# A mixture-of-experts layer on one core: the experts' combine with an unweighted one-hot, and rows in two fp32r parts

## The chip, the cores and the metric

The kernel runs as one program on one core of one Trainium2 chip. Five engines work side by side: TensorE (PE; its weight loads are listed as PEld), VectorE (DVE), ScalarE (ACT), GpSimd (POOL) and SyncE (SP), which in this kernel issues the transfers of weights. The metric is device time of one execution in microseconds (us), the median of several runs. All times below are from runs of this kernel or from the trace of one profiled execution.

## The reference, cut to what matters

One transformer layer on 256 tokens of width 2048, in fp32: a token mixer (window attention and a gated delta rule), then a hierarchical mixture of 32 experts, of which each token uses two. The mixer is not touched by the change. Of the experts this matters:

```python
combine = jnp.sum(jax.nn.one_hot(expert_idx, N_EXPERTS) * weights[..., None], axis=1)   # 256 x 32
y = jnp.zeros((n, d), jnp.float32)
for e in range(N_EXPERTS):
    gate, up = jnp.split(t @ w_gate_up[e], 2, axis=-1)                                   # 2048 -> 2 x 512
    y = y + combine[:, e:e + 1] * ((jax.nn.silu(gate) * up) @ w_down[e])                 # 512 -> 2048
x = layer_norm(ALPHA * x + g2 * y, ln2_g, ln2_b)
```

## The kernel before, in words

The experts are worked on in 16 pairs, one after the other. Each expert has 64 slots for tokens, so a pair fills the 128 partitions. For each pair TensorE does this:

- `gather`: the normalized rows of the pair's tokens, `xh`, are fetched into slots by a product with a one-hot matrix `G` (token by slot, two tiles of 128 tokens). The results `xg` become `XT` on ACT and DVE.
- `gate_up`: 16 loads of weights of 1 MB, `w_gu`; for each the products `pg` and `pu`, at line 1161, four records each. (A plain fp32 product shows as two records in the trace.)
- `turned`: `hs` = silu(gate) x up is turned around (`ht`, then copied to `hT`).
- `down`: 8 loads of 1 MB, `w_dn`, in four chunks `c` of 512 columns, two loads each. The product `pd` (line 1197) is followed by `dn` = `pd` x `g2b` on DVE (line 1201, `g2b` is the row g2), and by the combine: for each of the two token tiles the product `cb` (line 1207) of `GT` and `dn`, which DVE adds to `x` (line 1211, for the first pair 1209).
- `back`: `GT` is the transposed one-hot, in which each one is the token's weight: `Gw` = `G` x `comb` on DVE (line 1128), turned by TensorE (`gt`, line 1129), copied to SBUF (line 1130).

A chunk's combine isn't emitted right behind its `pd`: `down` appends it to the list `pend`, and `settle()` emits it behind the next chunk's `pd`, the last chunk's in the next pair's `gate_up`. The next pair's `gather` and `back` stand between `gate_up` and `down`. A scheduler then mixes neighbouring steps a little, and fixes the order of each engine. Each engine does its instructions in that order.

The loads go through SP's one queue into 17 buffers of 1 MB: 4 of the tile `w` (line 77), 6 of `w2` (line 1224) and 7 of `w1` (line 1239), in turn. SP issues a load when the buffer's last product is done. A pair needs 24 loads. In the first two stages of the kernel, before about 860 us, weights are split in two fp32r parts and multiplied in three products (`mm3`, lines 267 to 269); `mx` is one of their outputs. `last_rows` (line 1330) sets up the final layer norm's rows `l` during the last pair. If an expert has more than 64 tokens, a loop behind the pairs works them off (`overflow`).

Of the kernel before, what the change touches and what calls it, by code (L numbers as in the profile page):

```python
# [9 lines left out]
F32 = mybir.dt.float32  # L10
F32R = mybir.dt.float32r
AF = mybir.ActivationFunctionType
ALU = mybir.AluOpType
AX = mybir.AxisListType
PSUM = bass.MemoryType.PSUM

P = 128
D = 2048
KT = D // P
S = 256  # L20
NT = S // P
# [4 lines left out]
NE = 32  # L26
# [3 lines left out]
CAP = 64  # L30
# [36 lines left out]
def tile_block(ctx: ExitStack, tc: tile.TileContext, A: dict, out: bass.AP, dbg=None, upto=99):  # L67
# [40 lines left out]
    ident, ones = C("ident"), C("ones")  # L108
# [247 lines left out]
    def hilo(h, lo, src):  # L356
        SC.copy(h, src)
        V.tensor_tensor(lo, src, h.bitcast(F32), op=SUB)
# [725 lines left out]
    def weights():  # L1084
# [10 lines left out]
        V.tensor_add(o1, o1, o2)  # L1095
        over_groups(comb, o1)

    cnt = mo.tile([P, NE], F32, name="cnt")
    cmax = mo.tile([P, 1], mybir.dt.int32, name="cmax")
    cmaxf = mo.tile([P, 1], F32, name="cmaxf")  # L1100
# [13 lines left out]
    def slots(pr, pos2):  # L1114
        Gs = []
        for t in range(NT):
            Gt = mo.tile([P, 2, CAP], F32, tag=f"G{t}", name=f"G{pr}_{t}")
            V.tensor_tensor(Gt, pos2[:, t, :].unsqueeze(2).to_broadcast([P, 2, CAP]),
                            C("iom").unsqueeze(1).to_broadcast([P, 2, CAP]), op=ALU.is_equal)
            Gs.append(Gt)  # L1120
        return Gs

    def back(pr, Gs, comb2):
        GT = mo.tile([P, NT, P], F32, tag="GT", name=f"GT{pr}", bufs=2)
        p = pm(f"gt{pr}")
        for t in range(NT):
            Gw = mo.tile([P, 2, CAP], F32, tag=f"Gw{t}", name=f"Gw{pr}_{t}")
            V.tensor_tensor(Gw, Gs[t], comb2[:, t, :].unsqueeze(2).to_broadcast([P, 2, CAP]), op=MUL)
            T.transpose(p[:, t * P:(t + 1) * P], Gw.rearrange("p e s -> p (e s)"), ident)
        V.tensor_copy(GT, p[:, :S].rearrange("p (t s) -> p t s", t=NT))  # L1130
        return GT

    def gather(pr, Gs):
        XT = mo.tile([P, KT, P], F32, tag="XT", name=f"XT{pr}")

        def step(kq):
            p = pm(f"xg{pr}_{kq}")
            for k in range(4):
                for t in range(NT):
                    T.matmul(p[:, k * P:(k + 1) * P], xh[t][:, (4 * kq + k) * P:(4 * kq + k + 1) * P],  # L1140
                             Gs[t].rearrange("p e s -> p (e s)"), start=(t == 0), stop=(t == NT - 1))
            for k in range(4):
                K = 4 * kq + k
                if kq % 2:
                    V.tensor_scalar(XT[:, K, :], p[:, k * P:(k + 1) * P], sc2c[:, K:K + 1], sh2c[:, K:K + 1],
                                    op0=MUL, op1=ADD)
                else:
                    SC.activation(XT[:, K, :], p[:, k * P:(k + 1) * P], AF.Identity, bias=sh2c[:, K:K + 1],  # L1148
                                  scale=sc2c[:, K:K + 1])
        return XT, step  # L1150
# [32 lines left out]
    def settle():  # L1183

        while pend:
            pend.pop(0)()

    def down(pr, hT, GT, load):

        for c in range(4):  # L1190
            cs = slice(c * 512, (c + 1) * 512)
            pd = ps_d.tile([P, 512], F32, tag="d", name=f"pd{pr}_{c}")
            for fh in range(2):
                we = load(c, fh)
                for f in (2 * fh, 2 * fh + 1):
                    for e in range(2):
                        T.matmul(pd[64 * e:64 * e + 64, :], hT[:, f, 64 * e:64 * e + 64],  # L1197
                                 we[:, (2 * (f % 2) + e) * 512:(2 * (f % 2) + e + 1) * 512],
                                 start=(f == 0), stop=(f == 3))
            dn = mo.tile([P, 512], F32, tag="dn", name=f"dn{pr}_{c}", bufs=2)  # L1200
            V.tensor_tensor(dn, pd, g2b[:, cs], op=MUL)  # L1201
            settle()

            def add(c=c, cs=cs, dn=dn):
                for t in range(NT):
                    p = pm(f"cb{pr}_{c}{t}")
                    T.matmul(p, GT[:, t, :], dn, start=True, stop=True)  # L1207
                    if pr == 0:
                        V.scalar_tensor_tensor(x[t][:, cs], x[t][:, cs], ALPHA, p, op0=MUL, op1=ADD)
                    else:  # L1210
                        V.tensor_tensor(x[t][:, cs], x[t][:, cs], p, op=ADD)  # L1211
                    if pr == NE // 2 - 1:
                        V.bn_stats(sd[:, t, c, :], x[t][:, cs])

            pend.append(add)
# [39 lines left out]
        return w  # L1255

    def pair(pr):
        return pos[:, :, 2 * pr:2 * pr + 2], comb[:, :, 2 * pr:2 * pr + 2]

    def overflow():  # L1260
        NU = 3 * (NE // 2)
        ov = mo
        rp = ov.tile([P, NT, 3 * NE], F32, name="ov_pos")
        rc = ov.tile([P, NT, 3 * NE], F32, name="ov_comb")
        need = ov.tile([P, NU], F32, name="ov_need")
        pc = ov.tile([P, NE // 2], F32, name="ov_pc")
        V.tensor_reduce(pc, cnt.rearrange("p (a b) -> p a b", b=2), axis=AX.X, op=ALU.max)
        for r in range(3):
            V.tensor_scalar(rp[:, :, NE * r:NE * (r + 1)], pos, float(CAP * (r + 1)), None, op0=ALU.subtract)
            V.tensor_copy(rc[:, :, NE * r:NE * (r + 1)], comb)  # L1270
            V.tensor_scalar(need[:, 16 * r:16 * r + 16], pc, float(CAP * (r + 1)), None, op0=ALU.is_gt)
        pf = [ov.tile([P, NU], F32, name=f"ov_pf{j}") for j in range(2)]
        V.tensor_copy(pf[0], need)
        for j in range(6):
            d = 1 << j
            a, b = pf[j % 2], pf[(j + 1) % 2]
            V.tensor_copy(b[:, :d], a[:, :d])
            V.tensor_tensor(b[:, d:], a[:, d:], a[:, :NU - d], op=ALU.add)
        incl, eq = pf[0], pf[1]
        nn = ov.tile([P, 1], mybir.dt.int32, name="ov_n")  # L1280
        V.tensor_copy(nn, incl[:, NU - 1:NU])
        V.tensor_tensor(incl, incl, need, op=ALU.subtract)
        pid = C("pid")
        V.tensor_scalar(eq, incl, pid, None, op0=ALU.is_equal)
        V.tensor_tensor(eq, eq, need, op=ALU.mult)
        V.tensor_tensor(eq, eq, C("iota")[:, :NU], op=ALU.mult)
        col = ov.tile([P, 32], F32, name="ov_col")
        V.tensor_reduce(col[:, 0:1], eq, axis=AX.X, op=ALU.add)
        V.tensor_copy(col[:, 1:32], col[:, 0:1].to_broadcast([P, 31]))
        p = pm("ov_row")  # L1290
        T.matmul(p[:32, :P], col, ident, start=True, stop=True)
        lu = ov.tile([32, P], F32, name="ov_lu")
        lp = ov.tile([32, P], F32, name="ov_lp")
        lui = ov.tile([32, P], mybir.dt.int32, name="ov_lui")
        lpi = ov.tile([32, P], mybir.dt.int32, name="ov_lpi")
        V.tensor_copy(lu, p[:32, :P])
        V.tensor_scalar(lp, lu, 16.0, -16.0, op0=ALU.is_ge, op1=ALU.mult)
        V.tensor_add(lp, lp, lu)
        V.tensor_scalar(lu, lp, 16.0, -16.0, op0=ALU.is_ge, op1=ALU.mult)
        V.tensor_add(lp, lp, lu)  # L1300
        V.tensor_copy(lui, p[:32, :P])
        V.tensor_copy(lpi, lp)
        n = nc.values_load(nn[0:1, 0:1], min_val=0, max_val=NU)
        with tc.For_i(0, n, 1) as i:
            u = nc.values_load(lui[0:1, ds(i, 1)], engines=[mybir.EngineType.DVE], min_val=0, max_val=NU - 1)
            q = nc.values_load(lpi[0:1, ds(i, 1)], engines=[mybir.EngineType.SP], min_val=0, max_val=NE // 2 - 1)
            p2_ = ov.tile([P, NT, 2], F32, name="ov_p2")
            c2_ = ov.tile([P, NT, 2], F32, name="ov_c2")
            V.tensor_copy(p2_, rp[:, :, ds(u * 2, 2)])
            V.tensor_copy(c2_, rc[:, :, ds(u * 2, 2)])  # L1310
            Gs = slots("ov", p2_)
            XT, step = gather("ov", Gs)
            for kq in range(4):
                step(kq)
            GT = back("ov", Gs, c2_)
            hs = gate_up("ov", XT, lambda k: wload_m(
                A["w_gu"][ds(q * 16 + k, 1)].rearrange("o p f -> (o p) f")))
            down("ov", turned("ov", hs), GT, lambda c, fh: wload_m(
                A["w_dn"][ds(q * 8 + (2 * c + fh), 1)].rearrange("o p f -> (o p) f")))
            settle()  # L1320
        for t in range(NT):
            for c in range(4):
                V.bn_stats(sd[:, t, c, :], x[t][:, c * 512:(c + 1) * 512])
# [168 lines left out]
```

## Time and profile before

| | |
|---|---|
| median of 3 runs | 1871.32 us (1870.62 to 1871.38) |
| the profiled execution | 1872.44 us |
| its span in the trace | 1870.6 us |
| TensorE busy | 1785.3 us, 95% of the span |
| DVE busy / ACT busy | 870.9 us / 479.1 us |
| transferred | 628.56 MB, mean 336 GB/s |

The profiled execution's own time is 1.8 us above its span, and 1.1 us above the median. A busy TensorE is not a TensorE at its peak: records of products that follow each other overlap, and only the distance from one start to the next tells what a product costs.

### The profile page before, as it was taken

The page shows a single profiled execution, that of the slowest core. Times are in us where ns is not written, and L with a number is a line of the kernel's source. Part 1 is how long each engine was busy: PE and PEld are TensorE (multiplying, and loading weights), DVE is VectorE, ACT ScalarE, POOL GpSimd, SP SyncE. Part 2 cuts the span into 40 slices and gives each one's busy share as a digit, 9 for nine tenths or more (in the row PEclk, how much of TensorE's full clock was granted, in tenths as well). Part 3 has the DMA queues.
Part 4 walks back from the last instruction along what each step waited for, and adds up shares of the span by engine and source line. Part 5 has one row for each costly group of instructions (what it writes and reads, how often), then busy time and mean ns, then how long its engine had stood idle before and what let it go on. Part 6 is the DMA issues. An engine that isn't in the chain of part 4 may idle for free. (4 is left out here: it accounts for less than half of the span.)

```text
span 1870.6 us, 27302 instructions
## 1 busy us (share of the span) xinstructions
PE 1785.3 (95%) x11514; PEld 1120.0 (60%) x11514; DVE 870.9 (47%) x1375; ACT 479.1 (26%) x891; POOL 42.0 (2%) x47
## 2 busy tenths in 40 slices
PE   5999999999999999998999999999999999999995
PEld 2778988898999999885433444343433434343431
DVE  2355898788778788666212221122112221122115
ACT  2433698336233544435100000000000000000010
POOL 1000001102000000000000000000000000000000
PEclk8999999999999999998999999999999999999998
DMA  8887565455877688977999999999999999999953
GB/s 347 314 331 294 203 254 219 170 214 204 293 269 272 225 300 304 359 283 301 388 394 420 421 420 421 420 420 421 420 421 420 420 420 419 420 419 421 419 225 134
DMA packets 87286, 628.56 MB, mean 336 GB/s; under 512 B 9828, under 2 KB 9828, under 8 KB 11252
## 3 DMA queue, kind: packets, MB, share of 16 engines
q1 hardware_dynamic: 86832, 626.42, 84.3%
q8 instruction: 92, 1.51, 0.3%
q10 hardware_dynamic: 328, 0.36, 0.1%
q14 instruction: 34, 0.28, 0.0%
HBM read 624.64 MB, written 2.10 MB: 335 GB/s over the span
## 5 line engine op out<-in xcount | busy, mean ns | idle before, releaser
L262 ACT CAST wh<-w 128x1024 fp32r<-128x1024 f32 x216 | 225.8, 1050 | 311.3 <-PE ws L268 105.8
L263 DVE TENSOR_TENSOR wl<-w,wh 128x1024 fp32r<-128x1024 f32 x216 | 264.8, 1226 | 84.0 <-PE mx L268 22.8
L1161 PE MATMUL pg<-w,XT 128*64 128x512 f32 x1024 | 268.0, 600 | 0.2 <-ACT XT L1148 0.2
L1161 PE MATMUL pu<-w,XT 128*64 128x512 f32 x1024 | 264.0, 592 | 0.0
L267 PE MATMUL ws<-uh,wh 128*128 128x256 f32 x896 | 261.1, 291 | 1.1 <-ACT wh L262 1.1
L269 PE MATMUL ws<-uh,wl 128*128 128x256 f32 x896 | 253.9, 284 | 4.5 <-DVE wl L263 4.2
L268 PE MATMUL ws<-ul,wh 128*128 128x256 f32 x896 | 253.3, 283 | 0.0
L1197 PE MATMUL pd<-w,hT 128*64 128x512 f32 x1016 | 232.1, 598 | 0.8 <-DVE hT L1176 0.8
L1168 DVE TENSOR_TENSOR hs<-hs,pu 128x512 f32<-128x512 f32 x16 | 11.0, 688 | 420.2 <-PE pu L1161 420.2
L1167 ACT ACTIVATE hs<-pg 128x512 f32<-128x512 f32 x16 | 9.6, 597 | 756.5 <-PE pg L1161 756.5
L267 PEld LDWEIGHTS ws<-uh,wh 128*128 128x128 f32 x896 | 169.6, 189 | 11.5 <-issue 7.5
L269 PEld LDWEIGHTS ws<-uh,wl 128*128 128x128 f32 x896 | 169.6, 189 | 8.3 <-DVE wl L263 6.7
L268 PEld LDWEIGHTS ws<-ul,wh 128*128 128x128 f32 x896 | 169.7, 189 | 0.5 <-issue 0.5
L207 DVE SCALAR_TENSOR_TENSOR acc<-w,csil,acc 128x1024 f32<-128x1024 f32 x128 | 164.4, 1300 | 11.9 <-DMA w<-in_w_ada 11.7
L1161 PEld LDWEIGHTS pu<-w,XT 128*64 128x64 f32 x1024 | 73.8, 137 | 146.5 <-issue 146.5
L1197 PEld LDWEIGHTS pd<-w,hT 128*64 128x64 f32 x1016 | 67.3, 136 | 148.4 <-issue 124.7
L1161 PEld LDWEIGHTS pg<-w,XT 128*64 128x64 f32 x1024 | 68.0, 137 | 139.7 <-issue 135.8
L1140 PEld LDWEIGHTS xg<-G,xh 128*128 128x128 f32 x1024 | 120.2, 195 | 32.1 <-issue 25.0
L1207 PE MATMUL cb<-dn,GT 128*128 128x512 f32 x256 | 131.3, 625 | 3.6 <-DVE dn L1201 3.6
L1140 PE MATMUL xg<-G,xh 128*128 128x128 f32 x1024 | 129.3, 283 | 3.2 <-DVE hT L1176 0.8
L1211 DVE TENSOR_TENSOR x<-x,cb 128x512 f32<-128x512 f32 x120 | 82.6, 689 | 92.9 <-PE cb L1207 92.9
L1201 DVE TENSOR_TENSOR dn<-pd,g2b 128x512 f32<-128x512 f32 x64 | 44.3, 692 | 134.3 <-PE pd L1197 134.3
(354 smaller groups left out, 2148.8 us busy)
## 6 DMA issues: line engine op xcount, KB each, us to landing
w<-in_w_gu SPq DMA_DIRECT2D x256, 1024.0 KB, 13.0
w<-in_w_dn SPq DMA_DIRECT2D x127, 1024.0 KB, 9.7
w<-in_w_ada SPq DMA_DIRECT2D x64, 1024.0 KB, 4.9
w<-in_w_in SPq DMA_DIRECT2D x56, 1024.0 KB, 5.1
w<-in_w_a SPq DMA_DIRECT2D x32, 1024.0 KB, 7.3
w<-in_w_kq SPq DMA_DIRECT2D x20, 1024.0 KB, 6.9
w<-in_w_pab SPq DMA_DIRECT2D x16, 1024.0 KB, 6.7
w<-in_w_out SPq DMA_DIRECT2D x16, 1024.0 KB, 5.6
```

What stands on the lines that cost most here:

```text
L207: V.scalar_tensor_tensor(acc[:, hc], w[:, hc], csil[:, k:k + 1], acc[:, hc], op0=MUL, op1=ADD)
L262: SC.copy(h, w)
L263: V.tensor_tensor(lo, w, h.bitcast(F32), op=SUB)
L267: T.matmul(p, a[0], b[0], start=first, stop=False)
L268: T.matmul(p, a[0], b[1], start=False, stop=False)
L269: T.matmul(p, a[1], b[0], start=False, stop=last)
L1140: T.matmul(p[:, k * P:(k + 1) * P], xh[t][:, (4 * kq + k) * P:(4 * kq + k + 1) * P], Gs[t].rearrange("p e s -> p (e s)"), start=(t == 0), ...
L1161: T.matmul(dst[64 * e:64 * e + 64, :], XT[:, k, 64 * e:64 * e + 64], we[:, e * 1024 + hv * 512:e * 1024 + hv * 512 + 512], start=(k == 0), ...
L1197: T.matmul(pd[64 * e:64 * e + 64, :], hT[:, f, 64 * e:64 * e + 64], we[:, (2 * (f % 2) + e) * 512:(2 * (f % 2) + e + 1) * 512], start=(f = ...
L1201: V.tensor_tensor(dn, pd, g2b[:, cs], op=MUL)
L1207: T.matmul(p, GT[:, t, :], dn, start=True, stop=True)
L1211: V.tensor_tensor(x[t][:, cs], x[t][:, cs], p, op=ADD)
```

## The change

The one-hot `G` is made as fp32r, and stays unweighted when it is turned, so `Gw` falls away. fp32r is fp32 rounded to what one pass of TensorE takes. The weights reach the slots otherwise: `comb` is split once in two fp32r parts (`combp`), and for each pair a small product of `G` and the pair's four columns of `combp` gives the weight of each slot, which DVE sums to the column `ws`. In `down`, DVE multiplies `pd` in place, in PSUM, by `ws` and `g2b`. The result is split: ACT writes the rounded part `dh`, DVE the rest `dl` = `pd` - `dh`, both fp32r and with one buffer each. The combine is then two fp32r products, of `GT` with `dh` and with `dl`, summed in PSUM, where one plain fp32 product stood. The overflow loop gets the same.

```diff
+    def cut_weights(dst, src):
+        SC.copy(dst[:, :, :, 0, :], src)
+        V.tensor_tensor(dst[:, :, :, 1, :], src, dst[:, :, :, 0, :].bitcast(F32), op=SUB)
...
-            Gt = mo.tile([P, 2, CAP], F32, tag=f"G{t}", name=f"G{pr}_{t}")
+            Gt = mo.tile([P, 2, CAP], F32R, tag=f"G{t}", name=f"G{pr}_{t}")
...
-        GT = mo.tile([P, NT, P], F32, tag="GT", name=f"GT{pr}", bufs=2)
+        GT = mo.tile([P, NT, P], F32R, tag="GT", name=f"GT{pr}", bufs=2)
+        ws = mo.tile([P, 1], F32, tag="wsl", name=f"wsl{pr}", bufs=2)
         p = pm(f"gt{pr}")
         for t in range(NT):
-            Gw = mo.tile([P, 2, CAP], F32, tag=f"Gw{t}", name=f"Gw{pr}_{t}")
-            V.tensor_tensor(Gw, Gs[t], comb2[:, t, :].unsqueeze(2).to_broadcast([P, 2, CAP]), op=MUL)
-            T.transpose(p[:, t * P:(t + 1) * P], Gw.rearrange("p e s -> p (e s)"), ident)
+            T.transpose(p[:, t * P:(t + 1) * P], Gs[t].bitcast(F32), ident)
+        pw = p[:, S:S + 4]
+        for t in range(NT):
+            T.matmul(pw, Gs[t], cut[:, t], start=(t == 0), stop=(t == NT - 1))
         V.tensor_copy(GT, p[:, :S].rearrange("p (t s) -> p t s", t=NT))
+        for e in range(2):
+            r = slice(CAP * e, CAP * e + CAP)
+            V.tensor_reduce(ws[r], pw[r, e::2], axis=AX.X, op=ADD)
...
-            dn = mo.tile([P, 512], F32, tag="dn", name=f"dn{pr}_{c}", bufs=2)
-            V.tensor_tensor(dn, pd, g2b[:, cs], op=MUL)
+            V.scalar_tensor_tensor(pd, pd, ws, g2b[:, cs], op0=MUL, op1=MUL)
+            dh = mo.tile([P, 512], F32R, tag="dh", name=f"dh{pr}_{c}")
+            dl = mo.tile([P, 512], F32R, tag="dl", name=f"dl{pr}_{c}")
             settle()
+            hilo(dh, dl, pd)
...
                     p = pm(f"cb{pr}_{c}{t}")
-                    T.matmul(p, GT[:, t, :], dn, start=True, stop=True)
+                    T.matmul(p, GT[:, t, :], dh, start=True, stop=False)
+                    T.matmul(p, GT[:, t, :], dl, start=False, stop=True)
```

`hilo(h, lo, src)` was there before: `SC.copy(h, src)`, then `V.tensor_tensor(lo, src, h, op=SUB)`.

On TensorE, in the `down` of a middle pair, where `cb_10` is the combine of chunk 1 for token tile 0 and the last number of a name is its buffer; a row x3 stands for three more products on the same load. Before, from the end of chunk 1's `pd` to the start of chunk 3's:

```order
L1207 MATMUL cb_00_10682<-dn_0_10665,GT_10385 128x512 [waits DVE_49]
L1207 MATMUL cb_01_10685<-dn_0_10665,GT_10385 128x512 [waits PE_49]
L1197 MATMUL pd_2_10688<-w_10689,hT_10602 64x512 [waits DMAHW0_49,PE_49]
L1197 MATMUL pd_2_10688<-w_10689,hT_10602 64x512 x3
L1197 MATMUL pd_2_10688<-w,hT_10602 64x512 [waits DMAHW1_49]
L1197 MATMUL pd_2_10688<-w,hT_10602 64x512 x3
L1207 MATMUL cb_10_10703<-dn_1_10680,GT_10385 128x512 [waits DVE_49]
L1207 MATMUL cb_11_10706<-dn_1_10680,GT_10385 128x512 [waits DVE_49]
L1197 MATMUL pd_3_10709<-w,hT_10602 64x512 [waits DMAHW2_49,PE_49]
```

With the change, in the same place:

```order
L1225 MATMUL cb_00_11075<-dh_0_11055,GT_10752 128x512 [waits Activation_49]
L1226 MATMUL cb_00_11075<-dl_0_11056,GT_10752 128x512 [waits DVE_49]
L1225 MATMUL cb_01_11079<-dh_0_11055,GT_10752 128x512 [waits PE_49]
L1226 MATMUL cb_01_11079<-dl_0_11056,GT_10752 128x512
L1213 MATMUL pd_2_11085<-w_11086,hT_10990 64x512 [waits DMAHW0_49,PE_49]
L1213 MATMUL pd_2_11085<-w_11086,hT_10990 64x512 x3
L1225 MATMUL cb_10_11101<-dh_1_11073,GT_10752 128x512 [waits DVE_49,Activation_49]
L1213 MATMUL pd_2_11085<-w_11092,hT_10990 64x512 [waits DMAHW1_49]
L1213 MATMUL pd_2_11085<-w_11092,hT_10990 64x512 x3
L1226 MATMUL cb_10_11101<-dl_1_11074,GT_10752 128x512 [waits DVE_49]
L1225 MATMUL cb_11_11105<-dh_1_11073,GT_10752 128x512
L1226 MATMUL cb_11_11105<-dl_1_11074,GT_10752 128x512
```

Each combine product is now two, which wait for ACT (`dh`) and DVE (`dl`), and one of chunk 1 stands between the two loads of chunk 2. Further on, chunk 2's four stand between the two loads of chunk 3, as one of two did before, and chunk 3's four behind the next pair's first `pg` and `pu`, where one of its two stood.

On DVE, from chunk 1 of a middle pair to its end. Before:

```order
L1201 TENSOR_TENSOR dn_1_11712<-pd_1_11699,g2b 128x512
L1211 TENSOR_TENSOR x_8194<-x_8194,cb_00_11714 128x512
L1211 TENSOR_TENSOR x_8195<-x_8195,cb_01_11717 128x512
L1201 TENSOR_TENSOR dn_2_11733<-pd_2_11720,g2b 128x512
L1211 TENSOR_TENSOR x_8194<-x_8194,cb_10_11735 128x512
L1211 TENSOR_TENSOR x_8195<-x_8195,cb_11_11738 128x512
```

With the change:

```order
L1216 SCALAR_TENSOR_TENSOR pd_1_9943<-pd_1_9943,wsl_9637,g2b 128x512 [waits PE_49]
L1230 TENSOR_TENSOR x_8194<-x_8194,cb_00_9959 128x512 [waits PE_49]
L1230 TENSOR_TENSOR x_8195<-x_8195,cb_01_9963 128x512 [waits PE_49]
L358 TENSOR_TENSOR dl_1_9958<-pd_1_9943,dh_1_9957 128x512 [waits Activation_49]
L1216 SCALAR_TENSOR_TENSOR pd_2_9969<-pd_2_9969,wsl_9637,g2b 128x512 [waits PE_49]
L1230 TENSOR_TENSOR x_8194<-x_8194,cb_10_9985 128x512 [waits PE_49]
L1230 TENSOR_TENSOR x_8195<-x_8195,cb_11_9989 128x512 [waits PE_49]
L358 TENSOR_TENSOR dl_2_9984<-pd_2_9969,dh_2_9983 128x512 [waits Activation_49]
L1230 TENSOR_TENSOR x_8194<-x_8194,cb_20_10011 128x512 [waits PE_49]
L1230 TENSOR_TENSOR x_8195<-x_8195,cb_21_10015 128x512 [waits PE_49]
L1216 SCALAR_TENSOR_TENSOR pd_3_9995<-pd_3_9995,wsl_9637,g2b 128x512 [waits PE_49]
L358 TENSOR_TENSOR dl_3_10010<-pd_3_9995,dh_3_10009 128x512 [waits Activation_49]
```

`dl` of chunks 1 and 2 stands behind the two additions of the chunk ahead; `dl` of chunks 0 and 3 directly behind its own multiplication. SP's loads come in the same order as before.

## Rows read from the trace of the kernel before

**Rows 1.** The page's 40 slices: busy tenths of TensorE and of the DMA engines.
```profile
PE   5999999999999999998999999999999999999995
DMA  8887565455877688977999999999999999999953
```

**Rows 2.** Two stretches of the experts, by windows.
```profile
core 0: us, PE busy (x) PEld busy (x) DVE busy (x) ACT busy (x) POOL busy (x), PEclk, DMA share, GB/s
900.00:960.00 60.00, 59.81 (x294) 25.86 (x292) 16.37 (x39) 4.70 (x10) 0.00 (x0) 1.00 0.95 382
...
1260.00:1320.00 60.00, 59.00 (x280) 23.61 (x278) 13.55 (x27) 3.60 (x9) 0.00 (x0) 1.00 1.01 421
```

**Rows 3.** The page's groups: count, busy us, mean ns, idle before and releaser.
```profile
L1161 PE MATMUL pg<-w,XT 128*64 128x512 f32 x1024 | 268.0, 600 | 0.2 <-ACT XT L1148 0.2
L1197 PE MATMUL pd<-w,hT 128*64 128x512 f32 x1016 | 232.1, 598 | 0.8 <-DVE hT L1176 0.8
```

**Rows 4.** One load: its issue on SP, and its time from issue to landing.
```profile
1718.55 0.33 SPq L1224 DMA_DIRECT2D w<-in_w_gu  x1
...
w<-in_w_gu SPq DMA_DIRECT2D x1, 1024.0 KB, 14.1
```

**Rows 5.** TensorE's timeline: `pg` of pair 14's last two `w_gu` loads, start and us.
```profile
1754.84 1.03 PE L1161 MATMUL pg<-w,XT 128*64 128x512 f32 x4
...
1756.55 1.03 PE L1161 MATMUL pg<-w,XT 128*64 128x512 f32 x4
...
1759.30 0.66 PE L1174 MATMUL ht<-cst,hs 128*128 128x128 f32 x4 [0.86 <-DVE hs L1168]
```

**Rows 6.** TensorE's timeline in a middle pair, end of `down`.
```profile
1302.46 1.12 PE L1207 MATMUL cb<-dn,GT 128*128 128x512 f32 x2
1303.51 1.94 PE L1197 MATMUL pd<-w,hT 128*64 128x512 f32 x8
1305.38 1.99 PE L1207 MATMUL cb<-dn,GT 128*128 128x512 f32 x4
1307.30 1.08 PE L1161 MATMUL pg<-w,XT 128*64 128x512 f32 x4
...
1309.17 1.12 PE L1207 MATMUL cb<-dn,GT 128*128 128x512 f32 x2
```

**Rows 7.** TensorE's timeline in the mixer: fp32r products of the same shape.
```profile
765.05 0.39 PE L269 MATMUL mx<-wh,ml 128*128 128x512 f32 x1
765.28 0.39 PE L267 MATMUL mx<-wh,mh 128*128 128x512 f32 x1
```

**Rows 8.** Small products: `pbr` by its line (ns), `xg` and `gt` by timeline.
```profile
L906 PE MATMUL pbr<-mod,rin x32: 174/174/195, 788.0 to 789.1; 128*36 128x2 f32 x32
...
1280.36 5.62 PE L1140 MATMUL xg<-G,xh 128*128 128x128 f32 x48
1285.82 0.41 PE L1129 MATMUL gt<-cst,Gw 128*128 128x128 f32 x2
```

**Rows 9.** Work of 512 columns out of PSUM: DVE by line, ACT by line.
```profile
L1209 DVE SCALAR_TENSOR_TENSOR x<-x,cb x8: 687/689/689, 936.2 to 951.8; 128x512 f32<-128x512 f32 x8
...
L1330 ACT COPY l<-l x8: 585/585/593, 1795.7 to 1808.9; 128x512 f32<-128x512 f32 x8
```

**Rows 10.** The last combine, by timeline: TensorE, then DVE.
```profile
1849.57 1.08 PE L1197 MATMUL pd<-wl,hT 128*64 128x512 f32 x4
1851.74 1.98 PE L1207 MATMUL cb<-dn,GT 128*128 128x512 f32 x4 [1.09 <-DVE dn L1201]
...
1851.01 0.67 DVE L1201 TENSOR_TENSOR dn<-pd,g2b 128x512 f32<-128x512 f32 x1
1852.91 0.69 DVE L1211 TENSOR_TENSOR x<-x,cb 128x512 f32<-128x512 f32 x1 [1.22 <-PE cb L1207]
```

**Rows 11.** Early waits for weights: TensorE's timeline, and the window's granted clock.
```profile
29.32 1.06 PE L179 MATMUL fa<-w,crep 128*32 128x512 f32 x8 [1.25 <-DMA w<-in_w_a]
33.19 1.93 PE L179 MATMUL fa<-w,crep 128*32 128x512 f32 x8 [2.81 <-DMA w<-in_w_a]
...
30.00:40.00 10.00, 6.05 (x28) 2.21 (x24) 0.35 (x2) 0.58 (x1) 0.00 (x0) 0.58 1.01 422
```

More of the change, by code (lines that the diff above doesn't have):

```diff
@@ L1096, in weights @@
         over_groups(comb, o1)
+        cut_weights(combp, comb.rearrange("p t (q e) -> p t q e", e=2))
+    def cut_weights(dst, src):
+        SC.copy(dst[:, :, :, 0, :], src)
+        V.tensor_tensor(dst[:, :, :, 1, :], src, dst[:, :, :, 0, :].bitcast(F32), op=SUB)
+    combp = mo.tile([P, NT, NE // 2, 2, 2], F32R, name="combp")
     cnt = mo.tile([P, NE], F32, name="cnt")
@@ L1116, in slots, with back @@
         for t in range(NT):
-            Gt = mo.tile([P, 2, CAP], F32, tag=f"G{t}", name=f"G{pr}_{t}")
+            Gt = mo.tile([P, 2, CAP], F32R, tag=f"G{t}", name=f"G{pr}_{t}")
             V.tensor_tensor(Gt, pos2[:, t, :].unsqueeze(2).to_broadcast([P, 2, CAP]),
                             C("iom").unsqueeze(1).to_broadcast([P, 2, CAP]), op=ALU.is_equal)
-            Gs.append(Gt)
+            Gs.append(Gt.rearrange("p e s -> p (e s)"))
         return Gs
-    def back(pr, Gs, comb2):
-        GT = mo.tile([P, NT, P], F32, tag="GT", name=f"GT{pr}", bufs=2)
+    def back(pr, Gs, cut):
+        GT = mo.tile([P, NT, P], F32R, tag="GT", name=f"GT{pr}", bufs=2)
+        ws = mo.tile([P, 1], F32, tag="wsl", name=f"wsl{pr}", bufs=2)
         p = pm(f"gt{pr}")
         for t in range(NT):
-            Gw = mo.tile([P, 2, CAP], F32, tag=f"Gw{t}", name=f"Gw{pr}_{t}")
-            V.tensor_tensor(Gw, Gs[t], comb2[:, t, :].unsqueeze(2).to_broadcast([P, 2, CAP]), op=MUL)
-            T.transpose(p[:, t * P:(t + 1) * P], Gw.rearrange("p e s -> p (e s)"), ident)
+            T.transpose(p[:, t * P:(t + 1) * P], Gs[t].bitcast(F32), ident)
+        pw = p[:, S:S + 4]
+        for t in range(NT):
+            T.matmul(pw, Gs[t], cut[:, t], start=(t == 0), stop=(t == NT - 1))
         V.tensor_copy(GT, p[:, :S].rearrange("p (t s) -> p t s", t=NT))
-        return GT
+        for e in range(2):
+            r = slice(CAP * e, CAP * e + CAP)
+            V.tensor_reduce(ws[r], pw[r, e::2], axis=AX.X, op=ADD)
+        return GT, ws
     def gather(pr, Gs):
@@ L1140, in step @@
                     T.matmul(p[:, k * P:(k + 1) * P], xh[t][:, (4 * kq + k) * P:(4 * kq + k + 1) * P],
-                             Gs[t].rearrange("p e s -> p (e s)"), start=(t == 0), stop=(t == NT - 1))
+                             Gs[t].bitcast(F32), start=(t == 0), stop=(t == NT - 1))
             for k in range(4):
@@ L1186, in settle, with down @@
             pend.pop(0)()
-    def down(pr, hT, GT, load):
+    def down(pr, hT, bk, load):
+        GT, ws = bk
         for c in range(4):
@@ L1199, in down, with add @@
                                  start=(f == 0), stop=(f == 3))
-            dn = mo.tile([P, 512], F32, tag="dn", name=f"dn{pr}_{c}", bufs=2)
-            V.tensor_tensor(dn, pd, g2b[:, cs], op=MUL)
+            V.scalar_tensor_tensor(pd, pd, ws, g2b[:, cs], op0=MUL, op1=MUL)
+            dh = mo.tile([P, 512], F32R, tag="dh", name=f"dh{pr}_{c}")
+            dl = mo.tile([P, 512], F32R, tag="dl", name=f"dl{pr}_{c}")
             settle()
-            def add(c=c, cs=cs, dn=dn):
+            hilo(dh, dl, pd)
+            def add(c=c, cs=cs, dh=dh, dl=dl):
                 for t in range(NT):
                     p = pm(f"cb{pr}_{c}{t}")
-                    T.matmul(p, GT[:, t, :], dn, start=True, stop=True)
+                    T.matmul(p, GT[:, t, :], dh, start=True, stop=False)
+                    T.matmul(p, GT[:, t, :], dl, start=False, stop=True)
                     if pr == 0:
@@ L1257, in pair @@
     def pair(pr):
-        return pos[:, :, 2 * pr:2 * pr + 2], comb[:, :, 2 * pr:2 * pr + 2]
+        return pos[:, :, 2 * pr:2 * pr + 2], combp[:, :, pr].rearrange("p t a e -> p t (a e)")
     def overflow():
@@ L1279, in overflow, with cut_ov @@
         incl, eq = pf[0], pf[1]
+        oc = ov.tile([P, NT, 1, 2, 2], F32R, name="ov_cut")
+        def cut_ov(w):
+            cut_weights(oc, w.unsqueeze(2))
+            return oc.rearrange("p t q a e -> p t (q a e)")
         nn = ov.tile([P, 1], mybir.dt.int32, name="ov_n")
@@ L1314, in overflow @@
                 step(kq)
-            GT = back("ov", Gs, c2_)
+            GT = back("ov", Gs, cut_ov(c2_))
             hs = gate_up("ov", XT, lambda k: wload_m(
```

## The prediction, as it stood before the changed kernel was run

> **What bounds the kernel now.** I read the page's slices first. From the eighteenth slice on, when the experts begin, TensorE and the DMA engines are both at nine tenths or more, almost to the end [rows 1]. Both can't be read as the bound from that, so I went to windows. In a middle stretch of 60 us the transfers move 421 GB/s with a DMA share of 1.01, and TensorE is busy for 59.0 us [rows 2]. 421 GB/s in 60 us is 24.1 loads of 1024 KB, so a pair with its 24 loads takes 60 us, and a load takes 2.49 us. The DMA engines have nothing left to give at that rate. But the groups say that TensorE's big products never wait for a transfer: idle before `pg` is 0.2 us over the whole run, before `pd` 0.8 us, and the releaser is no DMA [rows 3]. So TensorE sets the pace, and the transfers happen to need the same 60 us per pair.
>
> How far ahead are the loads? The last load but one of pair 14's `gate_up` is issued at 1718.55 and lands 14.1 us later, at 1732.7 [rows 4]. Its `pg` starts at 1754.84 [rows 5]: it has lain there for 22.2 us. The last load lands 2.5 us later, at 1735.1, and is used at 1756.55: 21.4 us. This load is the tightest of a pair, since `gate_up` uses one load per 1.72 us (1756.55 less 1754.84) and one arrives per 2.49 us; in `down` and around it the stock grows again. **So TensorE may get faster by a total of 21.4 us up to that point; beyond that it waits for weights.** That is the core of the forecast.
>
> **What the combine costs now.** A stretch of four `cb` records lasts 1.92 us to the next start (1305.38 to 1307.30), one of two records 1.05 us (1302.46 to 1303.51) [rows 6]. So a record costs 0.435 us, and a turn from the half-wide products to the full-wide ones and back costs 0.18 us. A pair has 8 combine products, 16 records, in five stretches: 16 x 0.435 + 5 x 0.18 = 7.86 us.
>
> **What it costs afterwards.** The mixer has fp32r products of the same shape, one record each, 0.23 us from start to start (765.05 to 765.28; over several rows 0.227) [rows 7]. 16 of them, again in five stretches by the order shown: 16 x 0.227 + 0.90 = 4.53 us. The difference is 3.33 us per pair.
>
> **What is added on TensorE.** Two small products for the slot weights, four columns each. No row shows them. Below: `pbr`, 32 records in 1.1 us, 0.035 us each. Above: the turned `gt`, two records in 0.34 us (1285.82 to 1286.16 in the same chain), 0.17 us each; `xg` lies between, 5.46 us for 48 [rows 8]. With a full weight load they are nearer to `xg`; I take 0.25 us for both (0.07 to 0.34).
>
> **Waits that the split brings.** `dl` needs the multiplication (DVE), the rounding (ACT) and the subtraction (DVE). Nearest rows: 0.69 us for DVE out of PSUM, 0.59 us for ACT [rows 9]; no row writes PSUM from DVE, and I take the same 0.69. Handing over takes 0.06 us (`dn` ends at 1851.68, `cb` starts at 1851.74) [rows 10], and DVE starts some 0.12 us after `pd` ends on TensorE. Count from the end of a chunk's `pd`:
> - Chunks 0 and 1: their products stand one or two loads of `down` later, 1.87 us each [rows 6]. No wait.
> - Chunk 2: `dl` stands behind two additions. Ready at 0.12 + 0.69 + 2 x 0.72 + 0.69 + 0.06 = 3.0 us. Asked for after three products (0.86), a load (1.87) and one `dh` product with its turn (0.41): 3.1 us.
> - Chunk 3: ready at 0.12 + 0.69 + 0.04 + 0.59 + 0.05 + 0.69 + 0.06 = 2.24 us; asked for after `pg` and `pu` (1.87, from 1307.30 to 1309.17) and 0.41: 2.28 us.
>
> Both just meet, with nothing to spare. I take 0.3 us of waits per pair. If each of the seven steps took 0.2 us longer, it would be 1.4; the lower bound is 0. `dh` and `dl` have one buffer each, but their readers end well ahead of the next chunk's writers in the same counting. What is removed on DVE (`Gw`) and added (two sums, one subtraction per chunk) is covered: DVE is busy for 13.6 us of 60 [rows 2]. Splitting `comb` once costs well under 1 us, beside pair 0's `gate_up`.
>
> **Net on TensorE:** 3.33 - 0.25 - 0.3 = 2.8 us per pair, with bounds 3.26 and 3.33 - 0.34 - 1.4 = 1.6.
>
> **The sum.** Up to the last load of pair 14's `gate_up` there are 14 combines: 14 x 2.8 = 39 us are offered. The stock gives 21.4 us, plus what the transfers themselves gain. From 900 to 960 us they moved only 382 GB/s [rows 2], 5.6 us less than 421 GB/s would have given, because buffers came free late; TensorE frees them up to 2.8 us earlier there, so I take 1.5 us (0 to 5.6). After that point TensorE is again the slower one: no wait for weights is left in pair 15, because the eight `last_rows` products stand in its `gate_up`. Pair 14's `down` gives its 2.8 us. Pair 15's gives 3.33 less some 0.4 of waits, and less the longer chain behind the last `pd`. There 0.59 + 0.69 + 0.1 us are new between multiplication and second product, of which the two `dh` products hide 0.45: 0.9 us. So 2.0 us.
>
> 21.4 + 1.5 + 2.8 + 2.0 = 27.7 us. Span 1870.6 - 27.7 = 1842.9; its execution was 1.8 us longer, 1844.7; the median shown lies 1.1 us under that execution: **1844 us** rounded. The stock runs out after (21.4 + 1.5) / 2.8 = 8 pairs or so.
>
> **The rivals.**
> 1. *Faster, but TensorE stays the bound to the end.* If waits eat more than half of the net gain, under 1.64 us per pair (22.9 / 14), the stock is never used up. At 1.0 us per pair: 16 us, 1855. For it: chunks 2 and 3 have no slack. Against: the five-stretch sum is large.
> 2. *The transfers have room.* Then all of TensorE's gain arrives: 15 x 2.8 + 2.0 = 44 us, 1827. Against: 421 GB/s in every full stretch, also in the early window with the granted clock at 0.58 (422) [rows 2, 11], and a share of 1.01. The Trainium skill, "DMA: Bandwidth & Descriptors", section "Where 436 GB/s comes from", puts the ceiling at 435.2 GB/s, by which a pair's loads would take an estimated 57.9 us and not 60, and the time would be some 1835 us. The trace nowhere reaches that.
> 3. *The clock falls when TensorE begins to wait.* A wait of 1.25 us for weights left eight records at 1.06 us; after one of 2.81 us the same eight took 1.93, and the stretch shows a granted clock of 0.58 [rows 11], that is mostly at 1.2 GHz. The waits I forecast are 2.49 - 1.72 = 0.77 us each, three or so in a row at the end of `gate_up`, then the 0.86 us ahead of `ht` [rows 5]. That is less than in either row, but they come together. A fall of some 10 us would cost 5 us; then TensorE needs over 60 us, the stock grows, and no more waits follow. So it costs about 5 us once: 1849. The Trainium skill, "TensorE: Matmul & The Clock Gate", section "HAM oscillation — how this bites in real kernels", speaks against a change like this one: waits for transfers in every round throttle the clock in every round. By the two rows it hangs on the length of the waits.
> 4. *No change:* the transfers are the bound already, and the gain on TensorE turns into waits at once. Against: 21.4 us of stock. 1871.
> 5. *Slower:* the chain of multiplication, two additions, rounding and subtraction, 3.5 us, is not covered, and TensorE stands still for it in each chunk. With one load (1.87) as cover, 1.6 us x 4 = 6.5 us per pair against 3.1 gained: 3.4 x 16 = 55 us, 1926. It decides at 3.1 us of new waits per pair, 0.77 per chunk. Against: by the order a chunk's products stand behind a load or more of other work.
>
> **Chances and range.** The forecast 0.58 (its own range 1838 to 1850: early term 0 to 5.6, net 1.6 to 3.3); rival 1 0.14, rival 2 0.07, rival 3 0.08, rival 4 0.06, rival 5 0.07. A measurement of this kernel can tell about 0.2% (3.7 us) from no change. Faster: 0.87, same 0.06, slower 0.07. The range leaves out rivals 2, 4, 5 and the far end of rival 1: 1836 to 1858.
>
> **What would show it.** Right: `cb` at 0.227 us from start to start; in the first eight pairs a pair shorter than 60 us on TensorE by 2.8 us; then `pg` and `pu` with the DMA as releaser at the end of `gate_up`; 421 GB/s throughout; the clock at 1.00. Wrong: `cb` waiting for DVE by more than 1 us per pair, a granted clock under 1 in the late pairs, or over 425 GB/s.

## The result, and the profile after

The changed kernel takes 1843.11 us (median of 4 runs, 1841.24 to 1845.04), the kernel before 1871.35 in the same comparison: a ratio of 0.9848, 95% interval 0.9836 to 0.9860. Forecast were 1844 us and 1836 to 1858. The profiled execution took 1841.24 us with a span of 1839.4 us; it is one of the quicker ones, 1.9 us under the median. So the traces differ by 31.2 us where the medians differ by 28.2, and about 3 us of what the traces show is spread between executions. Two versions further on had one execution each that took several times as long (7496.57 and 4658.98 us); their medians are of the other three.

The groups of the changed kernel's page (count, busy us, mean ns, idle before and releaser):

```profile
L1175 PE MATMUL pg<-w,XT 128*64 128x512 f32 x1024 | 278.3, 599 | 4.0 <-DMA w<-in_w_gu 3.6
...
L1213 PE MATMUL pd<-w,hT 128*64 128x512 f32 x1016 | 234.3, 600 | 0.8 <-DVE hT L1190 0.8
```

In [rows 3] no product of weights waited for a transfer. Now `pg` does, 3.6 us on TensorE's own row (a weight load that waits ahead of it is listed apart). The timeline of TensorE shows the two kinds of pair. In the middle, from one `ht` to the next:

```profile
1267.21 0.66 PE L1188 MATMUL ht<-cst,hs 128*128 128x128 f32 x4 [0.86 <-DVE hs L1182]
...
1325.08 0.66 PE L1188 MATMUL ht<-cst,hs 128*128 128x128 f32 x4 [0.86 <-DVE hs L1182]
```

and late:

```profile
1676.06 0.66 PE L1188 MATMUL ht<-cst,hs 128*128 128x128 f32 x4 [0.86 <-DVE hs L1182]
...
1730.47 1.08 PE L1175 MATMUL pg<-w,XT 128*64 128x512 f32 x4 [0.55 <-DMA w<-in_w_gu]
...
1732.97 1.08 PE L1175 MATMUL pg<-w,XT 128*64 128x512 f32 x4 [0.56 <-DMA w<-in_w_gu]
...
1735.77 0.65 PE L1188 MATMUL ht<-cst,hs 128*128 128x128 f32 x4 [0.86 <-DVE hs L1182]
```

A middle pair takes 57.87 us, against 59.96 before (`ht` at 1279.57 and 1339.53 in that trace). A late one takes 59.71 us, and its last loads come 2.50 us apart (1730.47 to 1732.97), the time that a load takes on the DMA engines. The windows over the same stretches (columns as in [rows 2]):

```profile
900.00:960.00 60.00, 58.42 (x300) 26.67 (x298) 18.28 (x43) 6.14 (x14) 0.00 (x0) 1.00 0.95 391
...
1260.00:1320.00 60.00, 58.63 (x292) 24.83 (x290) 15.72 (x31) 5.95 (x13) 0.00 (x0) 1.00 1.01 421
...
1620.00:1680.00 60.00, 57.29 (x283) 23.96 (x283) 15.85 (x33) 5.95 (x13) 0.00 (x0) 1.00 1.01 420
```

The transfers move 420 to 421 GB/s, as before the change; in the early stretch 391 in place of 382. TensorE's clock is granted in full, also where it waits. SP's queue shows who holds whom back. Its waits from 1500 to 1740 us (line, what it waited for: us, times, longest), before the change:

```profile
SPq L1224 <- PE pu L1161: 43.2, 26, 3.4
SPq L1239 <- PE pu L1161: 41.6, 26, 3.4
...
SPq L1239 <- DMA w<-in_w_gu: 2.8, 3, 1.4
```

and now:

```profile
SPq L1258 <- DMA w<-in_w_gu: 55.8, 26, 3.2
SPq L1243 <- DMA w<-in_w_gu: 47.9, 23, 2.1
...
SPq L1258 <- PE cb L1226: 1.0, 3, 0.4
```

Before, SP held loads back until TensorE freed a buffer. Late in the changed kernel it waits for earlier transfers; buffers are free. The waits for weights begin in pair 12: the distances from one `ht` to the next, up to those of pairs 12, 13 and 14, are 59.65, 59.87 and 59.71 us, 5.6 us over three times 57.87.

### The profile page after: what moved, and what is told of

The parts are those of the page before. It is cut to its first block, busy times and chain, and to the rows that moved or that the text cites. A ratio compares the mean times of both kernels' runs of the same rounds, so it can differ in the third digit from the quotient of the medians.

```text
span 1839.4 us, 27526 instructions
## 1 busy us (share of the span) xinstructions
PE 1746.7 (95%) x11546; PEld 1126.4 (61%) x11546; DVE 904.7 (49%) x1440; ACT 516.3 (28%) x956; POOL 42.0 (2%) x47
## 5 line engine op out<-in xcount | busy, mean ns | idle before, releaser
L1175 PE MATMUL pg<-w,XT 128*64 128x512 f32 x1024 | 278.3, 599 | 4.0 <-DMA w<-in_w_gu 3.6
L1175 PE MATMUL pu<-w,XT 128*64 128x512 f32 x1024 | 274.7, 592 | 0.0
L1175 PEld LDWEIGHTS pu<-w,XT 128*64 128x64 f32 x1024 | 77.5, 137 | 146.4 <-issue 146.4
L1175 PEld LDWEIGHTS pg<-w,XT 128*64 128x64 f32 x1024 | 72.3, 137 | 134.9 <-issue 112.1
L357 ACT CAST dh<-pd 128x512 fp32r<-128x512 f32 x64 | 37.5, 585 | 281.7 <-DVE pd L1216 160.7
L1216 DVE SCALAR_TENSOR_TENSOR pd<-pd,wsl,g2b 128x512 f32<-128x512 f32 x64 | 48.5, 758 | 104.6 <-PE pd L1213 104.6
L267 PE MATMUL wq<-uh,wh 128*128 128x256 f32 x320 | 91.5, 289 | 5.1 <-ACT wh L262 2.8
## 6 DMA issues: line engine op xcount, KB each, us to landing
w<-in_w_gu SPq DMA_DIRECT2D x256, 1024.0 KB, 19.8
w<-in_w_dn SPq DMA_DIRECT2D x127, 1024.0 KB, 19.8
```

Of the source, the lines that this page charges most:

```text
L267: T.matmul(p, a[0], b[0], start=first, stop=False)
L1175: T.matmul(dst[64 * e:64 * e + 64, :], XT[:, k, 64 * e:64 * e + 64], we[:, e * 1024 + hv * 512:e * 1024 + hv * 512 + 512], start=(k == 0), ...
L1216: V.scalar_tensor_tensor(pd, pd, ws, g2b[:, cs], op0=MUL, op1=MUL)
```

## The experiments

**Undo the two products, keep the rest.** All pairs use one plain fp32 product; the unweighted one-hot and `ws` stay. Where `plain` is false, the lines of the changed kernel stand.

```diff
+            plain = True
+            if plain:
+                dh = mo.tile([P, 512], F32, tag=("dh", "dl")[c % 2], name=f"dn{pr}_{c}")
+                dl = None
+                V.scalar_tensor_tensor(dh, pd, ws, g2b[:, cs], op0=MUL, op1=MUL)
+                settle()
...
+                    if dl is None:
+                        T.matmul(p, GT[:, t, :].bitcast(F32), dh, start=True, stop=True)
```

> Unweighted one-hot, slot weights by the small product and the scaling column stay; the combine is one plain fp32 product again, in all pairs. Three theories. Stock: before, TensorE sets the pace with weights lying ready some 21 us ahead; the change makes TensorE about 2.1 us per pair faster, it eats up the stock by pair 10 or 11, then waits for weights, and only what is saved in the last two pairs counts in full again. TensorE to the end: TensorE sets the pace in every pair, and the gain is the sum of 16 equal savings. Side effects: the gain comes from what fell away beside the products (the weighted one-hot on DVE, the changed order). Stock and TensorE to the end both expect 1871 plus 16 times 0.1 to 0.3 us of small products, 1873 to 1876, and combine products at 0.43 us per record. Side effects expects 1843 to 1850.

Measured: 1876.61 us (ratio to before 1.0027, 1.0016 to 1.0038). Its combine, in the page's form:

```profile
L1233 PE MATMUL cb<-dn,GT 128*128 128x512 f32 x256 | 131.2, 625 | 3.8 <-DVE dn L1220 3.8
```

So the other parts of the change give nothing by themselves; they cost some 5 us, 0.6 over the most expected (in the traces 0.11 us in a middle pair and 2.0 in the first). The whole gain is the products', with the order that the scheduler gives them. The side-effects theory falls.

**Take away still more of TensorE's work.** The second part of the rows is left out, so the output is computed from rounded rows.

```diff
-            hilo(dh, dl, pd)
...
+            SC.copy(dh, pd)
...
-                    T.matmul(p, GT[:, t, :], dh, start=True, stop=False)
-                    T.matmul(p, GT[:, t, :], dl, start=False, stop=True)
+                    T.matmul(p, GT[:, t, :], dh, start=True, stop=True)
```

> The second part of the rows is left out: no subtraction on DVE, and one fp32r product per token tile instead of two, so 8 products of 0.23 us fewer per pair (rows are used rounded only). Stock: TensorE could save another 2.0 to 2.5 us per pair, but from pair 6 or so on it waits for weights, and only pairs 14 and 15 and the shorter end count: 4 to 8 us faster than the changed kernel, 1836 to 1839, with more waits on the transfers of weights (over 20 us in all). TensorE to the end: 16 times 2.2, 35 us faster, 1808.

Measured: 1837.78 us (0.9831, 0.9811 to 0.9851). 128 products fewer, and 5.3 us, where 35 were to be had. The page's `pg` tells where the rest went:

```profile
L1175 PE MATMUL pg<-w,XT 128*64 128x512 f32 x1024 | 279.7, 602 | 33.0 <-DMA w<-in_w_gu 30.9 <-ACT XT L1162 2.1
```

Waits for weights on this row grew from 3.6 to 30.9 us. TensorE does not set the pace to the end.

**The plain combine in three pairs, at two places.** In the first diff `plain` is `pr in (8, 9, 10)` or `pr in (13, 14, 15)`; all other pairs are as in the changed kernel.

> The changed kernel, with the plain fp32 combine in pairs 8, 9 and 10 only. TensorE loses 3 times 2.35, 7 us, in the middle. Stock: the changed kernel wastes some 6 us of TensorE's saving in waits for weights up to pair 14; these shrink instead, 1843 to 1845. TensorE to the end: 1850.

Measured: 1843.07 us (0.9854, 0.9838 to 0.9870), which can't be told from the changed kernel. From one `ht` to the next the three plain pairs take 60.03, 60.08 and 60.08 us, 6.6 us over three times 57.87. The three distances behind them, in which the changed kernel waits for weights, are now 57.91, 57.86 and 58.57.

> The same three pairs' worth of plain combine, but in pairs 13, 14 and 15. Stock: pair 13 is partly absorbed by its waits for weights, pair 14 costs 2.3 us, pair 15 (with the end behind it) 4 to 6: 1850 to 1852. TensorE to the end: the same as with pairs 8 to 10, 1850. The two theories differ in the difference between this run and that one: 6 to 8 us by the first, 0 to 3 by the second.

Measured: 1851.27 us (0.9900, 0.9880 to 0.9920). The difference is 8.2 us, at the edge of the stock theory's 6 to 8 and far from 0 to 3. But the loss is not the same at both places. By the same distances pair 13 loses 0.3 us (60.03 for 59.71), as it had waited for weights anyway, pair 14 loses 2.2 (66.18 for 63.97), and the last pair 5.8 (45.5 from `ht` to the end for 39.7): there the plain combine also brings back waits for `dn`. So it is the run in the middle that carries the argument: there 6.6 us of TensorE's work can't be seen in the time.

**Fewer transfers, same work on TensorE.** Before and after, 22 loads per pair in pairs 0 to 14: loads 8 and 12 of `gate_up` are left out, and their products use the load ahead again, so `gate_up` computes something else. The count at which the ring `w` is left is lowered by the loads left out.

```diff
-        if nld[0] > 12 * NE - len(AHEAD) - 8 and ring is wload:
+        if nld[0] > 12 * NE - len(AHEAD) - 8 - 2 * (NE // 2 - 1) and ring is wload:
...
-        return wload2(A["w_gu"][pr * KT + k])
+        if pr < NP - 1 and k in (8, 12):
+            return kept[pr]
+        kept[pr] = wload2(A["w_gu"][pr * KT + k])
+        return kept[pr]
```

> The kernel before with 22 loads per pair instead of 24 in pairs 0 to 14: in gate_up the products of loads 8 and 12 use the load ahead of them once more, so two loads of 1 MB are left out (and the result of gate_up is another). The products are as many as before. Stock: the transfers did not limit the kernel before; time 1866 to 1871, and TensorE's pair stays at 60.0 us. If the transfers had been the bound: 30 loads of 2.49 us less, 75 us faster, until TensorE limits.

Measured: 1868.38 us (0.9981, 0.9970 to 0.9991). 30 loads of 2.49 us, 75 us of transfers, were worth 3 us; TensorE's middle pair kept its 59.97 us (`ht` at 1278.72 and 1338.69). In the traces the gain lies in pairs 1 to 3 (2.2 us) and in the last (1.4 us up to its `ht`), where other products now stand right ahead of `ht` and fill its wait of 0.86 us. The transfers did not bound the kernel before.

> The same two loads per pair left out of the changed kernel. Stock: TensorE no longer meets the transfers and runs at its own 57.9 us per pair all along: the waits for weights are gone, and the time is 5 to 10 us under the changed kernel, 1834 to 1838. TensorE to the end: no wait was there to be removed, 1843.

Measured: 1836.24 us (0.9813, 0.9797 to 0.9830), 6.9 us under the changed kernel; in the traces the waits of three late pairs, 5.6 us, are gone. The windows late in both (kernel before, then changed, each with 22 loads):

```profile
1620.00:1680.00 60.00, 59.00 (x282) 23.64 (x280) 13.55 (x27) 3.60 (x9) 0.00 (x0) 1.00 0.97 386
```

```profile
1620.00:1680.00 60.00, 58.63 (x295) 25.40 (x296) 17.29 (x36) 6.24 (x14) 0.00 (x0) 1.00 0.98 397
```

The transfers are under their 420 GB/s in both; TensorE goes at its own pace, in the second at 57.86 us for each late pair (`ht` at 1556.31 and 1614.17).

**Use the waits.** In the last pair TensorE sets the pace, and there stand the eight products of `last_rows`. They can be asked for in pair 10. Their two tiles take buffers of the ring `w`, so the ring must be left five pairs sooner.

```diff
-        if pr == NP - 1:
+        if pr == 10:
             l2g, l2b = last_rows(8), last_rows(12)
...
-        if nld[0] > 12 * NE - len(AHEAD) - 8 and ring is wload:
+        if nld[0] > 12 * NE - len(AHEAD) - 8 - 24 * 5 and ring is wload:
             ring = 1
```

> The changed kernel, with the eight products that set up the final norm's rows asked for in pair 10 instead of pair 15 (their two buffers leave the ring of loads five pairs sooner, so 13 buffers are left). They cost TensorE some 8 us. Stock: in pair 15 they stand in a stretch where TensorE sets the pace and cost 8 us there; at pair 10 they fill time in which TensorE would wait for weights before pair 14. The end then comes as early as pair 15's own loads allow, some 4 us: 1838 to 1840. TensorE to the end: the place doesn't matter, 1843. With 13 buffers too few for the transfers: slower than 1843.

Measured: 1847.21 us (0.9870, 0.9854 to 0.9887): slower than the changed kernel, where the stock theory had 1838 to 1840. The products did move (1469.6 to 1489.8 us). But the windows show a price at the change of rings:

```profile
1500.00:1560.00 60.00, 58.63 (x294) 24.82 (x292) 15.73 (x31) 5.95 (x13) 0.00 (x0) 1.00 0.87 356
```

60 x (1 - 356/420) = 9.1 us of transfers were lost there. The loads of ring `w` had been sent to `w1`, whose seven buffers had just been filled; a buffer came up again after 7 loads. Late in this kernel the transfers set the pace, so these 9 us are never made good. The next run keeps the order of the buffers:

```diff
         j = nld[0] % len(rings)
+        if nld[0] >= 14 * 17:
+            j = 4 + (nld[0] - 14 * 17) % 13
...
-        if nld[0] > 12 * NE - len(AHEAD) - 8 and ring is wload:
-            ring = 1
```

> The changed kernel with the eight products of the final norm's rows asked for in pair 10, as in the run before, but from pair 10 on the loads go round the 13 buffers of w2 and w1 in turn, so that each buffer is asked for again after 13 loads and not after 7. Stock: if the last attempt lost its gain because the transfers stood still at the change of rings (a stretch of 356 GB/s, 9 us), that stretch now stays at 420 GB/s, and the time is 1838 to 1840, 3 to 5 us under the changed kernel. If 13 buffers are too few in any order, or if the place of the eight products doesn't matter: 1843 or more.

Measured: 1839.49 us (1838.57 to 1839.72; 0.9829, 0.9816 to 0.9843). The same window:

```profile
1500.00:1560.00 60.00, 58.62 (x292) 24.81 (x290) 15.72 (x31) 5.94 (x13) 0.00 (x0) 1.00 1.01 420
```

No transfer is lost, and the version is 3.6 us under the changed kernel's median; its five runs all lie under that kernel's four, though the intervals of the two ratios overlap. As a control, the same edits in the kernel before:

> The same move of the eight products and the same ring of 13 buffers in the kernel before. Stock: here TensorE sets the pace everywhere, so the place of its work doesn't matter: 1871, unless 13 buffers hold too little for a stock of 21 us (then some us slower). If moving the products out of the last pair were a gain by itself: 1866.

Measured: 1873.71 us (1.0008, 0.9999 to 1.0017). There the move is worth nothing, as expected where TensorE sets the pace everywhere.

## Why the prediction was right

**The core held:** TensorE ahead of the change set the pace with weights in store; its saving counts until the store is used up, then only behind pair 14's `gate_up`. The start of pair 14's `down` can be read directly, before and after:

```profile
1765.89 7.09 PE L1197 MATMUL pd<-w,hT 128*64 128x512 f32 x32
```

```profile
1742.44 7.09 PE L1213 MATMUL pd<-w,hT 128*64 128x512 f32 x32
```

It comes 23.4 us sooner. The prediction's stock plus early term was 22.9. The transfers themselves gained 2.2 us up to there, where 1.5 had been taken: the last load but one of pair 14's `gate_up`, issued at 1710.61, landed 19.8 us later, at 1730.4, and was used at once (1730.47), against 1732.6 before. The early stretch has 1.3 us of that, 391 for 382 GB/s in 60 us. One reading was off, with nothing hanging on it: in [rows 1] both engines are at nine tenths from the twentieth slice on, not the eighteenth.

**The combine's products** were sized nearly right: 0.23 us from start to start. TensorE's timeline of the last stretch of a middle pair:

```profile
1293.67 0.51 PE L1225 MATMUL cb<-dh,GT 128*128 128x512 f32 x1
1294.29 0.50 PE L1226 MATMUL cb<-dl,GT 128*128 128x512 f32 x1
1294.63 0.40 PE L1225 MATMUL cb<-dh,GT 128*128 128x512 f32 x1
1294.86 0.40 PE L1226 MATMUL cb<-dl,GT 128*128 128x512 f32 x1
1295.57 0.49 PE L1154 MATMUL xg<-G,xh 128*128 128x128 f32 x2 [0.31 <-DVE x L1230]
```

**The waits were under-sized.** The net gain per pair is 59.96 - 57.87 = 2.1 us, not 2.8. The rows show one wait that the prediction did not have: the next pair's first `xg` follows `cb` at once, takes a PSUM buffer of the same two, and waits until DVE has added `cb` to `x`. From 1294.86 to 1295.57 are 0.71 us, where the same step at the end of the stretch ahead took 0.32 (1289.77 to 1290.09): 0.4 us per pair. Chunk 3's `dl` also came late: 1293.67 to 1294.29 is 0.62 us, where the step from `dh` to `dl` took 0.34 in the stretch ahead; that is the 0.3 us that was taken. All five stretches come to 5.5 us instead of 4.8 with that wait. One cause of a late `dl` is the multiplication by `ws` and `g2b`, 0.76 us, for which 0.69 had been taken from [rows 9]:

```profile
L1216 DVE SCALAR_TENSOR_TENSOR pd<-pd,wsl,g2b x64: 742/759/760, 932.7 to 1819.7; 128x512 f32<-128x512 f32 x64
```

The small weight products cost less than the 0.25 us taken: `gt` and they together take 0.46 us, from 1331.28 to 1331.74 on TensorE, where `gt` alone took 0.34 [rows 8]. Some 0.2 us more go to the next pair's 16 `xg` records in `gate_up`: they stand in three stretches now and take 2.4 us, from start to start, where two stretches took 2.2. At 2.1 us a pair, 14 pairs still offer 29 us, over the 22.9 needed; 23.4 arrived, and nearly all of the rest is the 5.6 us of waits for weights. So the smaller size changed only the pair in which the store ran out, pair 12 and not pair 8 or so. That the answer hardly depends on this size is what the run with the plain combine in pairs 8 to 10 shows.

**The last pair was under-sized the other way.** From `ht` to the end of the span it took 45.2 us before (1825.37 to 1870.6) and 39.7 after (1799.74 to 1839.4): 5.6 us less, where 2.0 was forecast. The two starts:

```profile
1825.37 0.66 PE L1174 MATMUL ht<-cst,hs 128*128 128x128 f32 x4 [0.86 <-DVE hs L1168]
```

```profile
1799.74 0.65 PE L1188 MATMUL ht<-cst,hs 128*128 128x128 f32 x4 [0.86 <-DVE hs L1182]
```

The prediction took the products' saving and added waits, but the last pair had waits of its own before, for `dn`:

```profile
1831.35 1.10 PE L1207 MATMUL cb<-dn,GT 128*128 128x512 f32 x2 [0.89 <-DVE dn L1201]
...
1838.03 1.12 PE L1207 MATMUL cb<-dn,GT 128*128 128x512 f32 x2 [0.79 <-DVE dn L1201]
...
1844.74 1.12 PE L1207 MATMUL cb<-dn,GT 128*128 128x512 f32 x2 [0.79 <-DVE dn L1201]
```

With the 1.09 us ahead of the last one [rows 10] they come to 3.6 us. After the change the scheduler puts the first chunk's products behind three loads in place of two, and the four products of chunks 0, 1 and 3 in one stretch each; two idle times of TensorE are left on these rows, 0.15 and 1.17 us:

```profile
1812.23 0.50 PE L1226 MATMUL cb<-dl,GT 128*128 128x512 f32 x1 [0.15 <-DVE dl L358]
...
1821.15 0.73 PE L1225 MATMUL cb<-dh,GT 128*128 128x512 f32 x2 [1.17 <-ACT dh L357]
```

These sizes make the traces' 31.2 us: 23.4, 2.2 in between (pair 14's `down`, forecast 2.8) and 5.6. So by the traces the forecast sum of 27.7 is 3.5 us short, about as much as the last pair was under-sized. The medians differ by 28.2 only because the execution traced before was 1.1 us slower than its median and the one traced after 1.9 quicker. The mechanism was right; that the total came out within half a microsecond is luck.

**The rivals.** That TensorE stays the bound to the end (1) is excluded by the run with one product and by the plain combine in pairs 8 to 10. Room in the transfers (2): no slice of any run's page is over 422 GB/s. The ceiling of 435.2 in the Trainium skill, "DMA: Bandwidth & Descriptors", section "Where 436 GB/s comes from", was not reached by any run here. The 1835 us estimated from that ceiling do not fit the prediction's own stock: loads of an estimated 57.9 us a pair against TensorE's forecast 57.2 would take some 10 us out of 21.4 in 14 pairs, and all of the gain would arrive, 1827. The clock (3): it stayed at 1.00 in the changed kernel's windows, also with waits of 0.55 us ahead of `pg`. The Trainium skill, "TensorE: Matmul & The Clock Gate", section "HAM oscillation — how this bites in real kernels", has a kernel whose waits for transfers throttle the clock in every round; that did not happen here. But waits for weights are not all that bears on the clock. In the run with 22 loads after the change, 1790 to 1800 us shows a granted clock of 0.83, that is partly at 1.2 GHz, without a wait for weights: six records of `last_rows`, of 16 rows each, stand right ahead of the last pair's `ht`, and a wait of 0.79 us behind it. The 24 `pd` records that follow took 6.81 us, where the changed kernel's took 5.37. No change (4) and slower (5) are excluded by the result; the chain of DVE, ACT and DVE cost tenths of a microsecond per pair, as the order had let expect.

## What to carry to other kernels

Two engines that are both at 100% are not both the bound: find how long each operand lies ready before it is used. That store is the most that speeding up the engine can bring ahead of the point where it runs out; work moved from behind that point into the waits ahead of it brings some more. When the bound changes hands in the middle of a kernel, an edit is worth what it saves in the part where its engine sets the pace: here a loss of 6.6 us in pairs 8 to 10 could not be seen in the time, while the same edit cost 2.2 us in pair 14 and 5.8 in the last. When buffers are taken out of a ring, keep the distance at which a buffer comes up again; the change of rings alone cost 9 us of transfers.

## What the runs showed of the hardware that was not expected

- With buffers free, the transfers still did not run further ahead: late in the changed kernel a load took 19.9 us from issue to landing, eight loads of 2.49 us, and SP waited for earlier transfers. Of the 17 buffers only some eight were then being filled. In the trace the loads report on eight semaphores in turn, and each load is issued when the one eight places before it has landed (one at 1718.06, after a landing at 1717.99). So the limit seen here is one of the program; how many loads the chip's queue would hold was not tried.
- DVE's multiplication by a column and a row, 512 columns out of PSUM, took 0.759 us in place in PSUM. The run with the plain combine wrote it to SBUF, in 0.751:

```profile
L1220 DVE SCALAR_TENSOR_TENSOR dn<-pd,wsl,g2b x64: 733/751/753, 934.2 to 1855.3; 128x512 f32<-128x512 f32 x64
```

So writing to PSUM costs 0.008 us. With a number in place of the column the operation took 0.688 (`L1209`, [rows 9]): most of the difference goes with the column, though no run changed that alone.
